# A hybrid decoder step on one core: the prompt's compressed rows computed ahead of the fourth gate chunk

## The chip, the cores and the metric

One core of one Trainium2 chip runs the whole kernel. The metric is the device time of one execution in microseconds; the kernel before takes 467.59 us (median of 3 runs, 466.97 to 469.56).

## The reference

One layer of a hybrid decoder, for a prompt of 512 tokens and for 8 sequences that decode one token each. Every token's row is normalised and multiplied by one matrix `w_in`; the columns feed a state-space head group (32 groups with a scan over time) and an attention head group (8 query heads, 2 key/value heads). The attention has three branches: over compressed rows, over selected blocks and over a sliding window. Both groups are gated, joined, and multiplied by an output matrix. The compressed rows are made thus:

```python
def compress(rows, pe, w1, b1, w2):
    B, L, G, HD = rows.shape
    ch = rows.reshape(B, L // CMP_STRIDE, CMP_STRIDE, G, HD)
    pe = pe.reshape(2, CMP_STRIDE, 1, HD)
    w1 = w1.reshape(2, CMP_STRIDE, HD, CMP_HID)
    pa = jnp.einsum('bnjgd,jdh->bngh', ch + pe[0], w1[0])
    pb = jnp.einsum('bnjgd,jdh->bngh', ch + pe[1], w1[1])
    hid = jax.nn.gelu(pa[:, :-1] + pb[:, 1:] + b1)
    return jnp.einsum('bngh,hd->bngd', hid, w2)
```

It is done once for the prompt's own keys and values, and once, with the same weights, for the 1024 past tokens of each of the 8 decode sequences, which lie in a paged cache and are fetched through a page table.

## The kernel before

**Stages.** The first phase (`dense` and `ssm_all`, merged) normalises the input and multiplies it by `w_in` in chunks: u, five chunks of queries, keys and values, and last four gate chunks (`gate_mm`, each of some 190 matmuls of 128x256 or 128x264, three matmuls to a product since both operands are split in a high and a low part). The state-space runs of four sequences' worth of groups (`ssm_run`, sq 0 to 3) lie among them; their last matmuls are L782 and L787, their transposes at the end L810 and L811. The second phase merges `prompt` (four query/key tiles, attention, the GLU of the state-space output) and `sample` (compression and attention for the decode sequences, in four pairs). The third is the output projection.

**What sets the order.** A tile scheduler places every engine's instructions from the program's order, which it takes as the priority, and from its own estimate of when operands and buffers come free. Each engine then runs its list strictly in order, and waits at the head of the list until the operands are there.

**The compression of the prompt** (`compress_prompt`) is the first thing that `sample` does. It loads the weights `W1r` (four tiles of 512 KB), splits them in `W1h` (a cast on ScalarE) and `W1l` (a subtraction on VectorE, 1024 columns each), reads the prompt's key and value rows back from the output in DRAM as `ch` (four loads, L1108), transposes them on TensorE (L1113, eight 128x128), copies them to `XP`, multiplies by `W1r` (L1123, 128 matmuls; `kd` 0 for keys, then `kd` 1 for values), adds a bias `hb`, takes a GELU (`gx`, with results in `hidp`) and multiplies by `w2` (L1133, L1141). `pen` (L1101 transposes it) is the position embedding, laid out behind the rows in `XP`.

**Shared buffers.** The raw weights `W1r` lie in the pool `ld` of four buffers. The cache gathers of the decode sequences (tile `kvg`, L1329, one indirect DMA each on GpSimd) take their buffers from the same pool, so that the first four gathers need the four `W1r` tiles read for the last time. Of a gathered page VectorE makes `xr`, GpSimd copies `Vs`, TensorE transposes the keys (L1338) and `xr` (L1348), which becomes `XT`; L1372 multiplies it by `W1h` and `W1l`. `gx` and the tile `qsv` share a pool of two buffers.

**The query/key tiles** (`qk_tile`): `qs` and `ks` are split (ScalarE and VectorE), transposed on TensorE (L995, L1002), and ScalarE writes them to `QT` and `KT`. `QB` and `KN` are the decode sequences' queries and keys (L967, L969; scores L1286), L1291 spreads the gates.

Of the kernel before, what the change touches and what calls it, by code (L numbers as in the profile page):

```python
# [8 lines left out]
F32 = mybir.dt.float32  # L9
F32R = mybir.dt.float32r  # L10
# [26 lines left out]
def hymba_step_kernel(  # L37
# [87 lines left out]
    def run(*gens):  # L125
        for g in gens:
            for _ in g:
                pass
# [768 lines left out]

    def ssm_all():
        tab = ssm_tables(0)
        yield 1  # L900
        for sq in range(4):
            nxt = ssm_tables(sq + 1) if sq < 3 else None
            yield 1
            ssm_run(sq, tab)
            tab = nxt
            yield 1
        ssm_states()

    def dense():
# [40 lines left out]
        yield 1  # L950
        run(gate_mm(2, Wg[2]))
        yield 1
        run(gate_mm(3, Wg[3]))

# [99 lines left out]


    cw = cache_win[0]

    def load_w1(tile_):

        r = [[tile_("W1r") for _ in range(2)] for _ in range(2)]  # L1060
        for kd in range(2):
            for a in range(2):
                nc.sync.dma_start(r[kd][a].rearrange("p (j h) -> p j h", h=128),
                                  cmp_w1[0, kd, 1024 * a:1024 * a + 1024].rearrange("(j r) h -> r j h", r=128))
        return r

    w2 = st([128, 2, 64], "w2", tag="pni")
    nc.sync.dma_start(w2, cmp_w2[0].rearrange("k h d -> h k d"))
    pen = k1("pen", 128, 32)
    nc.sync.dma_start(pen, cmp_pe[0].rearrange("k (a j) d -> (k a) (j d)", j=2))  # L1070
    hb = st([128, 2], "hb")
    GC = math.sqrt(2.0 / math.pi)

    def gelu2(out, pin, n, bias):

        xb, x2 = k3("gx"), k3("gx2")
        for kd in range(2):
            S.activation(xb[:, n * kd:n * kd + n], pin(kd), AF.Identity, bias=bias[:, kd:kd + 1])
        xx, yy = xb[:, :2 * n], x2[:, :2 * n]
        S.activation(yy, xx, AF.Square)  # L1080
        V.tensor_scalar(yy, yy, 0.044715, 1.0, op0=ALU.mult, op1=ALU.add)
        V.tensor_tensor(yy, yy, xx, op=ALU.mult)
        S.activation(yy, yy, AF.Tanh, scale=GC)
        V.scalar_tensor_tensor(out, yy, 1.0, xx, op0=ALU.add, op1=ALU.mult)


    kcT = st([128, 2, 2, 32], "kcT", F32R)
    vbd = st([128, 2, 4, 64], "vbd", tag="Dm")

    W1h = [[None] * 2 for _ in range(2)]  # L1090
    W1l = [[None] * 2 for _ in range(2)]

    def compress_prompt():
        W1r = load_w1(ld)
        for kd in range(2):
            for a in range(2):
                W1h[kd][a], W1l[kd][a] = wh("W1h"), wh("W1l")
                split(W1h[kd][a], W1l[kd][a], W1r[kd][a])
        peT = k1("peT", 32)
        p = pb("cmp")  # L1100
        T.transpose(p[:, :32], pen, ident[:32, :32])  # L1101
        V.tensor_copy(peT, p[:, :32])
        XPv = [k2("XP", 528).rearrange("p (j n) -> p j n", n=66) for _ in range(2)]
        for kd in range(2):
            V.tensor_copy(XPv[kd][:, :, 64:66], peT[:, 16 * kd:16 * kd + 16].rearrange("p (a j) -> p j a", j=8))
        ch = pt_("ch")
        for kg in range(4):
            nc.sync.dma_start(ch[32 * kg:32 * kg + 32].rearrange("p (j d) -> p j d", d=64),  # L1108
                              kvp_rows[:, 64 * kg:64 * kg + 64].rearrange("(c j) d -> c j d", j=16))
        for hf in range(2):  # L1110
            p = pb("cmp")
            for j in range(4):
                T.transpose(p[:, 128 * j:128 * j + 128], ch[:, 512 * hf + 128 * j:512 * hf + 128 * j + 128], ident)  # L1113
            for kd in range(2):
                V.tensor_copy(XPv[kd][:, 4 * hf:4 * hf + 4, 0:64],
                              p.rearrange("p (j k n) -> p j k n", k=2, n=64)[:, :, kd, :])
        ph = pb("cmp")
        for kd in range(2):
            for jp in range(8):
                for a in range(2):  # L1120
                    for c in range(2):
                        o = 128 * jp + 64 * c
                        T.matmul(ph[64 * c:64 * c + 64, 65 * kd:65 * kd + 65], W1r[kd][a][:, o:o + 64], XPv[kd][:, jp, a:a + 65],  # L1123
                                 start=(kd == 0 and jp == 0 and a == 0), stop=(jp == 7 and a == 1), skip_group_check=True,
                                 tile_position=(0, 64 * c))
            yield 1
        V.tensor_tensor(hb, ph[:, 64:130:65], b1T, op=ALU.add)
        hidp = k1("hidp")
        gelu2(hidp, lambda kd: ph[:, 65 * kd:65 * kd + 64], 64, hb)
        V.memset(vbd, 0.0)  # L1130
        pk = pb("cmp")
        for e in range(2):
            T.matmul(pk[64 * e:64 * e + 64, 0:64], w2[:, 0, :], hidp[:, 0:64], start=True, stop=True, tile_position=(0, 64 * e))  # L1133
# [624 lines left out]
```

## Time and profile before

| what | value |
|---|---|
| median of 3 runs | 467.59 us (466.97 to 469.56) |
| profiled execution | 468.64 us, span 466.9 us |
| mean granted TensorE clock | 0.985 |
| TensorE busy | 452.1 us (97%) |
| VectorE, ScalarE, GpSimd busy | 348.8, 241.3, 95.4 us |
| chain that ended last, by engine | PE 73%, DVE 13%, DMA 7%, POOL 3% |

Times are microseconds from the span's start. PE is TensorE's matmul stream, DVE VectorE, ACT ScalarE, POOL GpSimd, SP the engine that issues most DMAs. A row of a timeline gives the start, the time from there to the last end, engine, line, operation, tiles, the number of instructions, and in brackets the idle time of that engine just before it and what ended it. Matmuls overlap, so the times of rows next to each other do not add up to the stretch that they cover. The chain of waits is followed back from the last instruction; its pieces do add up.

### The profile page before, as it was taken

The page shows a single profiled execution, that of the slowest core. Times are in us where ns is not written, and L with a number is a line of the kernel's source. Part 1 is how long each engine was busy: PE and PEld are TensorE (multiplying, and loading weights), DVE is VectorE, ACT ScalarE, POOL GpSimd, SP SyncE. Part 2 cuts the span into 40 slices and gives each one's busy share as a digit, 9 for nine tenths or more (in the row PEclk, how much of TensorE's full clock was granted, in tenths as well). Part 3 has the DMA queues.
Part 4 walks back from the last instruction along what each step waited for, and adds up shares of the span by engine and source line. Part 5 has one row for each costly group of instructions (what it writes and reads, how often), then busy time and mean ns, then how long its engine had stood idle before and what let it go on. Part 6 is the DMA issues. An engine that isn't in the chain of part 4 may idle for free.

```text
span 466.9 us, 10954 instructions
## 1 busy us (share of the span) xinstructions
PE 452.1 (97%) x4258; PEld 385.9 (83%) x4258; DVE 348.8 (75%) x942; ACT 241.3 (52%) x587; POOL 95.4 (20%) x104
## 2 busy tenths in 40 slices
PE   8999999999999998799999999999899999999996
PEld 4989999899999998698686776867568799799885
DVE  6978999998998998385676858687756687683332
ACT  5913764756324328475676668566856555342100
POOL 3100000056442000462342214321433010000000
PEclk9999999999999997789999999999999999999999
DMA  8776533614627433466143362429343784311211
GB/s 290 247 225 167 84 73 108 187 40 82 143 57 214 129 82 73 148 209 187 46 140 114 121 215 79 148 90 350 104 141 130 220 209 152 101 58 58 69 46 48
DMA packets 75635, 62.84 MB, mean 135 GB/s; under 512 B 29262, under 2 KB 69056, under 8 KB 75456
## 3 DMA queue, kind: packets, MB, share of 16 engines
q1 hardware_dynamic: 66208, 36.74, 28.2%
q0 software_dynamic: 4816, 17.03, 11.5%
q10 hardware_dynamic: 4560, 8.39, 5.7%
q8 instruction: 33, 0.54, 0.5%
q14 instruction: 18, 0.15, 0.1%
HBM read 55.63 MB, written 10.70 MB: 142 GB/s over the span
## 4 chain that ended last, share of the span: by engine, by line
PE 73%; DVE 13%; DMA 7%; POOL 3%; issue 2%; ACT 1%; SPq 0%; DVEq 0%; POOLq 0%; ACTq 0%
PE a L121 11%; PE a L122 11%; PE a L123 10%; PE ph L1372 8%; DMA kvg<-in_cache_kv_dram,idx 4%; PE a L1262 4%; PE t L1253 4%; PE a L1220 3%; PE t L1348 3%; PE c L1545 3%; POOL rsq L168 2%; DVE ga L62 2%; PE t L1338 2%; PE ph L473 1%; DMA x<-in_x_prompt_dram 1%
## 5 line engine op out<-in xcount | busy, mean ns | idle before, releaser
L121 PE MATMUL a<-hTh,whi 128*128 128x256 f32 (+1 forms) x192 | 54.8, 287 | 0.6 <-DVE sg L61 0.6
L122 PE MATMUL a<-hTh,wlo 128*128 128x256 f32 (+1 forms) x192 | 54.8, 287 | 0.0
L123 PE MATMUL a<-hTl,whi 128*128 128x256 f32 (+1 forms) x192 | 53.4, 284 | 0.0
L1329 POOL DMA_INDIRECT kvg<-in_cache_kv_dram,idx x32 | 32.8, 1026 | 82.2 <-PE c L1123 40.1
L168 POOL TENSOR_TENSOR rsq<-rsq,mhalf 128x6 f32<-128x6 f32 (+3 forms) x10 | 28.7, 2872 | 101.8 <-DVE rsq L62 101.8
L122 PE MATMUL a<-whi,hTl 128*128 128x256 f32 (+1 forms) x160 | 45.8, 287 | 0.0
L123 PE MATMUL a<-wlo,hTh 128*128 128x256 f32 (+1 forms) x160 | 45.3, 284 | 0.0
L121 PE MATMUL a<-whi,hTh 128*128 128x256 f32 (+1 forms) x160 | 45.2, 287 | 0.0
L1372 PE MATMUL ph<-XT,W1h 128*128 128x256 f32 x256 | 44.5, 298 | 0.0
L61 ACT ACTIVATE P<-a,mx 128x128 f32<-128x128 f32 (+3 forms) x64 | 33.6, 533 | 13.3 <-DVE mx L61 11.5
L61 DVE TENSOR_REDUCE mx<-a 128x1 f32<-128x384 f32 (+3 forms) x48 | 27.9, 596 | 13.8 <-PE a L1221 13.6
L121 PEld LDWEIGHTS a<-hTh,whi 128*128 128x128 f32 x192 | 36.2, 188 | 1.1 <-DVE sg L61 0.8
L122 PEld LDWEIGHTS a<-hTh,wlo 128*128 128x128 f32 x192 | 36.2, 188 | 0.9 <-issue 0.4
L122 PE MATMUL a<-woh,mixl 128*128 128x256 f32 x128 | 36.1, 283 | 0.0
L121 PE MATMUL a<-woh,mixh 128*128 128x256 f32 x128 | 36.1, 284 | 0.0
L123 PE MATMUL a<-wol,mixh 128*128 128x256 f32 x128 | 36.0, 283 | 0.0
L123 PEld LDWEIGHTS a<-hTl,whi 128*128 128x128 f32 x192 | 35.7, 189 | 0.1
L1372 PEld LDWEIGHTS ph<-XT,W1h 128*128 128x128 f32 x256 | 34.9, 192 | 0.3 <-ACT XT L61 0.2
L62 ACT CAST whi<-w 128x1024 fp32r<-128x1024 f32 (+4 forms) x26 | 23.9, 927 | 15.8 <-PE a L122 10.5
L61 ACT COPY pT<-t 128x512 f32<-128x512 f32 x40 | 23.1, 588 | 15.8 <-PE t L1253 12.6
L122 PEld LDWEIGHTS a<-whi,hTl 128*128 128x128 f32 x160 | 30.1, 188 | 1.2 <-issue 0.9
L121 PEld LDWEIGHTS a<-whi,hTh 128*128 128x128 f32 x160 | 29.9, 189 | 0.9 <-PE ph L473 0.4
(410 smaller groups left out, 1235.5 us busy)
## 6 DMA issues: line engine op xcount, KB each, us to landing
w<-in_w_in_dram SPq DMA_DIRECT2D x16, 512.0 KB
out_dram<-in_cache_win_dram ACTq DMA_DIRECT2D x8, 511.0 KB
x<-in_x_prompt_dram SPq DMA_DIRECT2D x4, 512.0 KB
TT<-scr_k SPq DMA_DIRECT2D x4, 512.0 KB
w<-in_w_in_dram SPq DMA_DIRECT2D x16, 128.0 KB
W1r<-in_cmp_w_dram SPq DMA_DIRECT2D x4, 512.0 KB
wk<-in_cache_win_dram SPq DMA_DIRECT2D x8, 256.0 KB
wv<-in_cache_win_dram SPq DMA_DIRECT2D x8, 256.0 KB
```

The lines of the kernel that those rows point to most:

```text
L61: return f(*args, **kw)
L62: return f(*args, **kw)
L121: T.matmul(out, ah, bh, start=start, stop=False, skip_group_check=True)
L122: T.matmul(out, al, bh, start=False, stop=False, skip_group_check=True)
L123: T.matmul(out, ah, bl, start=False, stop=stop, skip_group_check=True)
L168: return G.tensor_tensor(out, out, mhalf[:parts, :cols], op=ALU.pow)
L1220: T.matmul(bank, QTv(g, r)[:, qsl], KTv(g, a)[:, brs, :n], start=(a == 0), stop=False, skip_group_check=True)
L1253: T.transpose(p[:, 128 * r:128 * r + 128], P[r][:, br, 128 * kt:128 * kt + 128], ident)
L1262: mm = T.matmul(po[64 * br:64 * br + 64, :], kvt[kt - 1][:, c0:c0 + 64], behind[kt - 1][br][0], start=(kt == 1), stop=(kt == i + 1), tile_ ...
L1329: G.indirect_dma_start(out=gt_, out_offset=None, in_=ckv, in_offset=bass.IndirectOffsetOnAxis(ap=idx[:, 2 * pr_ + b2, jq:jq + 1], axis=0))
L1348: T.transpose(p[:, 256 * g + 128 * b2:256 * g + 128 * b2 + 128], gts[jq][b2][:, o:o + 128], ident)
L1372: T.matmul(ph3[:, kd], (W1l if part == 1 else W1h)[kd][a][:, wsl], (xl if part == 2 else xh)[:, e, a:a + 256], start=(jq == 0 and kd == 0 ...
```

## The change

`load_w1`, `gelu2`, `compress_prompt`, the loads of `w2` and `pen` and their tiles stand ahead of `ssm_all` and `dense`. The splits are a function of their own, `w1_split`. `dense` loads `W1r` ahead of gate chunk 2, runs the compression to its end after that chunk, and splits the weights of `kd` 1 after gate chunk 3; those of `kd` 0 are split inside the compression, after its first 64 matmuls. `sample` takes three empty turns in its place. Nothing is computed that was not computed before. Lines of the changed kernel: L1093, L1100 were L995, L1002; L955 was L1113; L965 was L1123; L977, L985 were L1133, L1141; L1065, L1067 were L967, L969; L1291, L1296 were L1286, L1291; L1343, L1353, L1377 were L1338, L1348, L1372.

```diff
+    def w1_split(W1r, kd):
+        for a in range(2):
+            W1h[kd][a], W1l[kd][a] = wh("W1h"), wh("W1l")
+            split(W1h[kd][a], W1l[kd][a], W1r[kd][a])
+
+    def compress_prompt(W1r):
...
+        ph = pb("cmp")
+        for kd in range(2):
+            for jp in range(8):
+                for a in range(2):
+                    for c in range(2):
...
+            if kd == 0:
+                w1_split(W1r, 0)
+            yield 1
...
+        W1r = load_w1(ld)
         run(gate_mm(2, Wg[2]))
+        run(compress_prompt(W1r))
         yield 1
         run(gate_mm(3, Wg[3]))
+        w1_split(W1r, 1)
...
-    def compress_prompt():
-        W1r = load_w1(ld)
-        for kd in range(2):
-            for a in range(2):
-                W1h[kd][a], W1l[kd][a] = wh("W1h"), wh("W1l")
-                split(W1h[kd][a], W1l[kd][a], W1r[kd][a])
...
     def sample():
-        yield from compress_prompt()
+        yield 1
+        yield 1
+        yield 1
         for i in range(4):
             yield from sample_pair(i)
```

The diff does not tell where the scheduler puts the moved instructions. On TensorE around the transposes of `ch`, the list before (a row is line, operation, output and inputs with buffer numbers, size, and how many alike):

```order
L1002 MATMUL a_3000<-identr_303,ks_2988 128x128 x4
L1101 MATMUL c_2826<-cst_70,pen_2753 128x32
L995 MATMUL a_3037<-identr_303,qs_2985 128x128 x4
L1113 MATMUL c_2838<-cst_70,ch_2833 128x128 x4
L1113 MATMUL c_2845<-cst_70,ch_2833 128x128 x4
L1002 MATMUL a_3044<-identr_303,ks_2988 128x128 x4
L995 MATMUL a_3074<-identr_303,qs_3066 128x128 x4
L1123 MATMUL c_2852<-XP_2829,W1r_2801 64x65 x2
L1123 MATMUL c_2852<-XP_2829,W1r_2802 64x65 x2
```

And the list of the changed kernel, from the last matmul of gate chunk 3 (L123) on:

```order
L123 MATMUL a_2820<-hTl_115,whi_2469 128x264
L1093 MATMUL a_2957<-identr_303,qs_2949 128x128 x4
L1100 MATMUL a_2964<-identr_303,ks_2952 128x128 x4
L955 MATMUL c_2649<-cst_70,ch_2644 128x128 x3
L810 MATMUL t_2511<-cst_70,hfin_486 16x128
L811 MATMUL t_2511<-cst_70,hs_485 128x128
L810 MATMUL t_2511<-cst_70,hfin_486 16x128
L811 MATMUL t_2511<-cst_70,hs_485 128x128
L955 MATMUL c_2649<-cst_70,ch_2644 128x128
L955 MATMUL c_2656<-cst_70,ch_2644 128x128 x4
L1093 MATMUL a_2971<-identr_303,qs_2949 128x128 x4
L1100 MATMUL a_2978<-identr_303,ks_2952 128x128 x4
```

The first transposes of `ch` stand behind two groups of four transposes of the query/key tiles, in place of seven. Behind these rows come five more transposes of `qs` and `ks`, and then the 128 matmuls L965 in one piece. All of it still follows gate chunk 3; the state-space matmuls L782 and L787 of sq 3 now stand 33 matmuls ahead of that chunk's end.

On TensorE around the first gathered pages, the list before:

```order
L1002 MATMUL a_3081<-identr_303,ks_3069 128x128 x3
L995 MATMUL a_3092<-identr_303,qs_3066 128x128 x4
L1002 MATMUL a_3099<-identr_303,ks_3069 128x128 x4
L1338 MATMUL t_3013<-cst_70,kvg_3014 128x128 x2
L995 MATMUL a_3144<-identr_303,qs_3136 128x128 x4
L1348 MATMUL t_3030<-cst_70,xr_3017 128x128
L1002 MATMUL a_3151<-identr_303,ks_3139 128x128 x4
L1338 MATMUL t_3013<-cst_70,kvg_3021 128x128 x2
L995 MATMUL a_3166<-identr_303,qs_3136 128x128 x4
L1348 MATMUL t_3030<-cst_70,xr_3024 128x128
L1348 MATMUL t_3030<-cst_70,xr_3017 128x128
```

And that of the changed kernel:

```order
L1100 MATMUL a_3099<-identr_303,ks_3069 128x128 x4
L1093 MATMUL a_3144<-identr_303,qs_3136 128x128 x4
L1100 MATMUL a_3151<-identr_303,ks_3139 128x128 x4
L977 MATMUL c_2748<-hidp_2737,w_496 64x64 x2
L985 MATMUL c_2755<-w_496,hidp_2737 32x64 x8
L1093 MATMUL a_3166<-identr_303,qs_3136 128x128 x4
L1065 MATMUL t_2883<-cst_70,qsv_2884 128x8 x4
L1067 MATMUL t_2883<-cst_70,kvs 128x8 x2
L1343 MATMUL t_3013<-cst_70,kvg_3014 128x128 x2
L1343 MATMUL t_3013<-cst_70,kvg_3021 128x128 x2
L1100 MATMUL a_3173<-identr_303,ks_3139 128x128 x4
L1353 MATMUL t_3030<-cst_70,xr_3017 128x128
```

The query/key tiles that stood between and behind the `L1123` rows now follow `L965`, and the matmuls of `hidp` (L977, L985), which stood well behind the first L1372, stand ahead of the transposes of the gathered pages `kvg_3014` and `kvg_3021`.

On VectorE from the bias `hb` on, before:

```order
L61 TENSOR_TENSOR hb_2755<-c_2852,spT_320 128x2
L62 COPY xr_3017<-kvg_3014 128x2x4x64
L62 COPY xr_3024<-kvg_3021 128x2x4x64
L61 COPY kT_3028<-t_3013 128x512
L62 TENSOR_SCALAR gx_2956<-gx_2956 128x128
L62 TENSOR_TENSOR gx_2956<-gx_2956,gx_2955 128x128
L62 COPY xr_3110<-kvg_3107 128x2x4x64
L61 TENSOR_TENSOR XT_2789<-t_3030,XT_2787 128x2x256
L62 COPY xr_3117<-kvg_3114 128x2x4x64
L62 SCALAR_TENSOR_TENSOR hidp_2954<-gx_2956,gx_2955 128x128
```

And of the changed kernel:

```order
L61 TENSOR_TENSOR hb_500<-c_2663,spT_320 128x2
L62 COPY xr_3017<-kvg_3014 128x2x4x64
L62 COPY xr_3024<-kvg_3021 128x2x4x64
L62 TENSOR_TENSOR ks_3139<-kvt_312,ks_3139 128x2x128 x2
L62 TENSOR_SCALAR gx_2739<-gx_2739 128x128
L62 TENSOR_TENSOR gx_2739<-gx_2739,gx_2738 128x128
L62 SCALAR_TENSOR_TENSOR hidp_2737<-gx_2739,gx_2738 128x128
L62 COPY qsv_2884<-qsr_316 8x512
L62 MEMSET vbd_502 128x512
L61 COPY QB_2880<-t_2883 64x4x4 x4
L61 COPY KN_2882<-t_2883 128x16
```

The GELU's two steps and `hidp` still stand behind the copies `xr` of the first two gathered pages, but `qsv`, `vbd`, `QB`, `KN` and the key copy `kT` now stand behind `hidp`. On GpSimd the first four gathers come ahead of the copies `Vs`, and the fifth and sixth behind all four; on SP the four loads of `ch` keep their place among the stores `scr_y`. From the first L1372 of `jq` 2 on (at 213.36 us in the trace before) TensorE's list is the same in both kernels, and so it is on the other engines from about there.

## Rows read from the trace of the kernel before

**Rows 1.** The chain of waits around the phases' boundary: start, us on the chain, what.

```profile
177.92 0.61 DVE qs L62
...
187.59 1.14 PE c L1123 x32
...
188.94 2.97 PE c L1123 x96
...
192.17 5.88 DMA kvg<-in_cache_kv_dram,idx
...
204.16 0.27 PE c L1133 x4
204.42 0.38 PE c L1141 x16
```

**Rows 2.** Timeline of PE, 173 to 215 us.

```profile
175.20 2.16 PE L787 MATMUL t<-U,TT 128*64 128x72 f32 x32
178.58 0.54 PE L995 MATMUL a<-identr,qs 128*128 128x128 f32 x4 [1.22 <-DVE qs L62]
...
179.38 0.42 PE L1002 MATMUL a<-identr,ks 128*128 128x128 f32 x3
...
184.69 1.93 PE L1113 MATMUL c<-cst,ch 128*128 128x128 f32 x8
...
195.73 0.69 PE L1338 MATMUL t<-cst,kvg 128*128 128x128 f32 x2 [2.77 <-DMA kvg<-in_cache_kv_dram,idx]
...
200.90 0.91 PE L1372 MATMUL ph<-XT,W1h 128*128 128x256 f32 x4
...
213.36 0.72 PE L1372 MATMUL ph<-XT,W1h 128*128 128x256 f32 x4
```

**Rows 3.** Stretches: length, busy us of each engine, then PEclk (granted clock), DMA share.

```profile
181.00:187.30 6.30, 6.30 (x56) 5.93 (x54) 4.56 (x24) 5.38 (x19) 0.00 (x0) 0.50 0.23 49
187.30:195.00 7.70, 5.66 (x143) 5.19 (x141) 2.22 (x7) 3.51 (x14) 3.30 (x4) 0.94 0.29 82
195.00:201.20 6.20, 4.96 (x29) 4.78 (x30) 3.20 (x7) 3.20 (x10) 4.04 (x6) 0.50 0.75 251
201.20:213.40 12.20, 12.20 (x123) 11.14 (x121) 10.60 (x23) 7.69 (x23) 5.32 (x8) 0.99 0.66 198
```

**Rows 4.** Timelines of DVE, ACT and POOL, the same stretch.

```profile
176.71 1.22 DVE L62 TENSOR_TENSOR W1l<-W1r,W1h 128x1024 fp32r<-128x1024 f32 x1
...
188.61 0.75 DVE L62 TENSOR_TENSOR ks<-kvt,ks 128x256 fp32r<-128x256 f32 x2
...
198.07 0.43 DVE L62 COPY xr<-kvg 128x512 f32<-128x512 f32 x1 [1.94 <-DMA kvg<-in_cache_kv_dram,idx]
...
199.43 0.48 DVE L62 TENSOR_SCALAR gx<-gx 128x128 f32<-128x128 f32 x1
199.94 0.50 DVE L62 TENSOR_TENSOR gx<-gx,gx 128x128 f32<-128x128 f32 x1
...
201.78 0.48 DVE L62 SCALAR_TENSOR_TENSOR hidp<-gx,gx 128x128 f32<-128x128 f32 x1
```

```profile
193.25 0.66 ACT L61 CAST QT<-a 128x256 fp32r<-128x256 f32 x2
193.76 0.70 ACT L61 CAST KT<-a 128x256 fp32r<-128x256 f32 x2
...
200.95 0.33 ACT L62 ACTIVATE gx<-gx 128x128 f32<-128x128 f32 x1
```

```profile
190.78 1.09 POOL L1329 DMA_INDIRECT kvg<-in_cache_kv_dram,idx  x1 [40.12 <-PE c L1123]
192.17 0.96 POOL L1329 DMA_INDIRECT kvg<-in_cache_kv_dram,idx  x1 [0.30 <-DVE hb L61]
```

**Rows 5.** SP's queue at the boundary, and two direct loads on the chain.

```profile
174.67 2.70 SPq L1108 DMA_DIRECT2D ch<-out_dram  x3
```

```profile
147.03 4.14 DMA W1r<-in_cmp_w_dram
...
151.59 1.95 DMA out_dram<-kvt
```

More of the change, by code (lines that the diff above doesn't have):

```diff
@@ L895, in silu_gates, with load_w1 @@
             yield 1
+    cw = cache_win[0]
+    def load_w1(tile_):
+        r = [[tile_("W1r") for _ in range(2)] for _ in range(2)]
+        for kd in range(2):
+            for a in range(2):
+                nc.sync.dma_start(r[kd][a].rearrange("p (j h) -> p j h", h=128),
+                                  cmp_w1[0, kd, 1024 * a:1024 * a + 1024].rearrange("(j r) h -> r j h", r=128))
+        return r
+    w2 = st([128, 2, 64], "w2", tag="pni")
+    nc.sync.dma_start(w2, cmp_w2[0].rearrange("k h d -> h k d"))
@@ new lines, in hymba_step_kernel, with gelu2 @@
+    pen = k1("pen", 128, 32)
+    nc.sync.dma_start(pen, cmp_pe[0].rearrange("k (a j) d -> (k a) (j d)", j=2))
+    hb = st([128, 2], "hb")
+    GC = math.sqrt(2.0 / math.pi)
+    def gelu2(out, pin, n, bias):
+        xb, x2 = k3("gx"), k3("gx2")
+        for kd in range(2):
+            S.activation(xb[:, n * kd:n * kd + n], pin(kd), AF.Identity, bias=bias[:, kd:kd + 1])
+        xx, yy = xb[:, :2 * n], x2[:, :2 * n]
+        S.activation(yy, xx, AF.Square)
+        V.tensor_scalar(yy, yy, 0.044715, 1.0, op0=ALU.mult, op1=ALU.add)
+        V.tensor_tensor(yy, yy, xx, op=ALU.mult)
+        S.activation(yy, yy, AF.Tanh, scale=GC)
+        V.scalar_tensor_tensor(out, yy, 1.0, xx, op0=ALU.add, op1=ALU.mult)
@@ L1053, in glu @@
                 V.scalar_tensor_tensor(mixS[:, ct], th[:, 0:8], 0.25, sgS[0][:, ct], op0=ALU.mult, op1=ALU.mult)
-    cw = cache_win[0]
-    def load_w1(tile_):
-        r = [[tile_("W1r") for _ in range(2)] for _ in range(2)]
-        for kd in range(2):
-            for a in range(2):
-                nc.sync.dma_start(r[kd][a].rearrange("p (j h) -> p j h", h=128),
-                                  cmp_w1[0, kd, 1024 * a:1024 * a + 1024].rearrange("(j r) h -> r j h", r=128))
-        return r
@@ L1067, in hymba_step_kernel @@
[L1067 to L1084, printed above, removed]
@@ L1087, in hymba_step_kernel @@
[L1087 to L1091, printed above, removed]
-    def compress_prompt():
-        W1r = load_w1(ld)
-        for kd in range(2):
-            for a in range(2):
-                W1h[kd][a], W1l[kd][a] = wh("W1h"), wh("W1l")
-                split(W1h[kd][a], W1l[kd][a], W1r[kd][a])
[L1099 to L1133, printed above, removed]
-        kcs = k1("kcs", 64)
-        S.mul(kcs, pk[:, 0:64], 0.5)
-        V.tensor_copy(kcT[:, :, 0, :], kcs.rearrange("p (g c) -> p g c", g=2))
-        V.tensor_tensor(kcT[:, :, 1, :], kcs.rearrange("p (g c) -> p g c", g=2), kcT[:, :, 0, :].bitcast(F32), op=ALU.subtract)
-        pk = pb("cmp")
-        for r in range(4):
-            for g in range(2):
-                T.matmul(pk[32 * r:32 * r + 32, 64 * g:64 * g + 64], hidp[:, 64 + 32 * g:64 + 32 * g + 32], w2[:, 1, :],
-                         start=(g == 0), stop=(g == 1), skip_group_check=True, tile_position=(0, 32 * r))
-        for r in range(4):
-            sl = slice(32 * r, 32 * r + 32)
-            S.mul(vbd[sl, :, r, :], pk[sl, 0:128].rearrange("p (g d) -> p g d", g=2), 0.5)
-        yield 1
@@ L1671, in sample @@
     def sample():
-        yield from compress_prompt()
+        yield 1
+        yield 1
+        yield 1
         for i in range(4):
```

47 lines of the change are left out of this document (added).

## The prediction

> **What bounds the kernel now.** I read the chain of waits first. The change moves work at the boundary of the first two phases, and there the chain changes hands: VectorE's split `qs` [rows 1], then TensorE through L1123, then one gather of 5.88 us, then TensorE again to the end. The second view is TensorE's timeline: L787 ends the first phase at 175.20 + 2.16 = 177.36, the engine is idle for 1.22 us for `qs`, does transposes and L1123, is idle for 2.77 us for the second gathered page, and starts the first L1372 at 200.90 [rows 2]. The third is the table of stretches, for the clock: after each of these two idles the granted clock stood at 0.50, the lower level, first for 181.0 to 187.3, then for 195.0 to 201.2, and TensorE was busy in all or most of both [rows 3]. From 201.2 to 213.4 it is busy without a gap (12.20 of 12.20 us) at 0.99. The fourth is GpSimd's timeline: the first gather is issued at 190.78 after 40.12 us of idleness that L1123 ends, and the second at 192.17 [rows 4]. They wait for the weights' raw buffers.
>
> From the L1372 at 213.36 [rows 2] on the lists of both kernels agree and TensorE is full, so whatever is won or lost by then is carried to the end at about its size. The sum is therefore a question of one number: when the first L1372 (call it T0, 200.90 before) starts, and what work has by then been done in advance.
>
> **The change, step by step.**
>
> *The boundary.* One of the four splits `W1l` (1.22 us [rows 4]) no longer stands ahead of the first `qs` on VectorE. `qs` can be ready at about 177.3, when L787 and the gate matmuls end, and the 1.22 us of idleness shrink to 0 to 0.5. TensorE begins the query/key tile at 177.4 to 177.9 in place of 178.58. The split comes later, beside transposes; it gates only the later gathers.
>
> *The transposes of `ch`.* They now stand behind two groups of transposes. Twelve transposes took from 178.58 to 179.80 [rows 2], 0.1 each, so they are at the head of the queue at 178.2 to 178.7. The loads of `ch` keep their place: the three last are issued from 174.67 to 177.37 [rows 5], the last of them from about 176.5. The trace does not show when it lands. The nearest direct loads on the chain took 1.95 us (another small transfer) and 4.14 us (512 KB) [rows 5]; `ch` has a quarter of the bytes, so I take it near the lower, at 178.9, and keep 178.4 to 180.6. In the kernel before this landing was covered by seven us of other work (177.4 to 184.69 [rows 2]); that cover is gone. The wait at the head of the queue is then 0 to 2.4 us, and I take about 0.5.
>
> *L965.* From the first L1113 to the first L1123 the kernel before took 2.9 us, at the low clock [rows 1, 2]. After, 25 transposes at 0.1 lie there, and the copies to `XP`; I keep the 2.9. L965 starts at 181.8. The 32 matmuls took 1.14 us [rows 1], so the 64 of `kd` 0 end at 184.1 and all 128 near 186.
>
> *The gathers.* Before, the 64th matmul ended at 188.94 + 32 x 0.031 = 189.9, and the first gather followed at 190.78, 0.85 later, the second 1.39 after that [rows 1, 4]. After: 185.0 and 186.4. The second lands 5.88 later, at 192.2, against 198.05: the transfer that the kernel waits for is nearly 6 us earlier.
>
> *What is late next.* This gain doesn't reach T0. The matmuls of `hidp` (L977, L985) now stand ahead of the first page's transposes on TensorE, and `hidp` is made on VectorE behind the copies `xr` of the first two pages. After the landing at 192.2 follow xr 0.43, `ks` 0.75, gx 0.48 and 0.50, tanh 0.33 on ScalarE, hidp 0.48 [rows 4], 2.97 in all. L977 starts at 195.2, with both pages' transposes queued behind it, though the pages have long been there. TensorE has less than that to do: nine groups of transposes follow L965, which ScalarE empties at 0.51 a pair of copies [rows 4], so they end by about 190.8. Some four us of idleness remain until 195.2.
>
> *From L977 to T0.* 20 transposes at 0.1, 0.65 for L977 and L985 [rows 1], some 0.75 for the small matmuls of the decode queries and gates (an estimate: they are few, each below a transpose), 0.5 for the last copy to `XT`: 3.9 us at full clock, 199.1, and 3.4 more at half, 202.5. The rows say low: both idles above a microsecond were followed by a low stretch, which began 2.0 us (192.96 to 195.0) or 3.6 us (177.36 to 181.0) after the idle's start and lasted 6.2 or 6.3 us [rows 2, 3]. From an idle near 191 that is low from 193 to 194.6, until 199.2 to 200.9. L977 and what follows run at half until then. I take T0 = 201.0, with 199.9 to 202 as bounds.
>
> *The sum.* T0 moves by +0.1, and 0.65 for the `hidp` matmuls, which before came behind T0, is already done: -0.55. The sum stands against the profiled execution, 468.64 (span 466.9 and 1.74 around it): 468.1. That execution lies 1.05 above the median of the runs, so the forecast is 467.0; the bounds of T0 give 465.9 to 468.0. The moved small loads, the empty turns and the earlier `hfo`, `hso` copies cost nothing as long as TensorE's list covers them; if that cover goes, they are below half a microsecond each. A difference under 0.5% (2.34 us) is about what a measurement here can't tell from no change.
>
> **The rivals.**
>
> *A, faster: the clock is high when L977 comes.* The idle may be split up by the late `qs` and `ks` tiles, or the low stretch may end early. For it: 1.22 us of idleness at the boundary is gone, and with it, it may be, the first low stretch. Against it: both long idles of this trace cost a low stretch. Then T0 = 199.1, -1.8 - 0.65 = -2.45: 465.1, and down to 464 if gathers land faster than 5.88.
>
> *B, slower: `ch` lands late.* Place: the first L955, at the head of TensorE's list. If `ch` lands after about 179.9, TensorE idles for over 1.2 us, the idle that before was followed by 6.3 us at half [rows 2, 3]. Then L965's `kd` 0 takes 4.6 in place of 2.3, and with the wait the second gather lands 3.5 to 4.7 later, at 195.7 or after; L977 starts at 198.7, still behind `hidp`, and a second low stretch follows. T0 near 204.6: +3.7 - 0.65 = +3.0, 470.6. For it: a third of the landing's bounds lies beyond that point. Against it: the transfer is small.
>
> *C, slower: transposes do not hold the clock.* TensorE does 33 transposes between the gate chunk and L965 and some 35 after it. If they did not count as work, the clock would fall in the first of these stretches whatever `ch` does, and the time would be that of B, 470.6. The rows speak against it: the clock rose at 187.3 after 6.3 us of 56 matmuls that are nearly all transposes [rows 3]. The Trainium skill, TensorE: Matmul & The Clock Gate, Part 4 (PE-mode transpose), states that the full clock does not engage for transposes, since they are not counted as busy. By that rule the change would be slower; by the row, it is not decided by transposes, and this trace disagrees with the page.
>
> *D, nothing:* the scheduler keeps the compression behind gate chunk 3, so its words promise more than its list holds; if the gathers gain nothing either, 467.6.
>
> **How the numbers follow.** The forecast, -0.55, gets 0.45: every step rests on a row but the landing of `ch`. A gets 0.28, B 0.16, C 0.06, D 0.05. Faster by over 0.5% is A, 0.28; within is the forecast and D, 0.50; slower is B and C, 0.22. The range goes from within A (464.6) to B's time (470.6); left out are the far half of B and C and a tail of A. The likeliest case alone holds 465.9 to 468.0.
>
> **What would show it.** Right: the second gather issued near 186.4 and landing near 192; TensorE idle for some four us ahead of L977, released by `hidp`; a clock of 0.50 behind that; the first L1377 near 201. An idle ahead of L955 over 1.2 us and 0.50 during L965 would show B; the same without the idle, C. No idle ahead of L977 would make the whole sum wrong, and so would a stretch behind T0 where TensorE has gaps.

## The result, and the profile after

The changed kernel takes 470.87 us (median of 12 executions, 470.18 to 473.1), the kernel before 467.8 (12 executions, 465.68 to 469.56). The ratio is 1.0066, with a 95% interval of 1.0045 to 1.0087: slower by 3.1 us, where 0.55 faster was forecast, and outside the range. The time lies at that of the rivals B and C (470.6), but it will turn out that neither mechanism is what happened. Ratios, and the rows for the kernel before in the table below, leave out the few executions that took over 1.5% longer than the fastest of their kernel.

The chain of waits of the changed kernel around the boundary, the pieces that the prediction had priced:

```profile
172.99 3.25 DMA ch<-out_dram
...
185.60 6.06 DMA kvg<-in_cache_kv_dram,idx
...
192.98 0.15 DVE gx L62
193.15 0.38 DVE gx L62
193.55 0.32 ACT gx L62
193.89 0.30 DVE hidp L62
194.24 0.48 PE c L977 x4
```

By the chain one of the three late loads of `ch` landed at 172.99 + 3.25 = 176.24, and L955, which reads all four loads, did not wait at 177.85. The second gather was issued at 185.60 (forecast 186.4, before 192.17 [rows 4]) and took 6.06 us. From its landing the chain goes where the prediction put it: VectorE's steps to `hidp`, and L977 at 194.24 (forecast 195.2).

The timeline of TensorE:

```profile
176.62 0.28 PE L123 MATMUL a<-hTl,whi 128*128 128x264 f32 x1
176.97 0.54 PE L1093 MATMUL a<-identr,qs 128*128 128x128 f32 x4
...
177.85 0.52 PE L955 MATMUL c<-cst,ch 128*128 128x128 f32 x3
...
181.11 3.95 PE L965 MATMUL c<-XP,W1r 128*64 128x65 f32 x128
...
186.94 0.53 PE L1093 MATMUL a<-identr,qs 128*128 128x128 f32 x4 [0.79 <-ACT KT L61]
...
192.70 0.70 PE L1100 MATMUL a<-identr,ks 128*128 128x128 f32 x3 [1.25 <-DVE ks L62]
194.24 0.48 PE L977 MATMUL c<-hidp,w 128*64 128x64 f32 x4 [0.84 <-DVE hidp L62]
...
201.61 1.22 PE L1377 MATMUL ph<-XT,W1h 128*128 128x256 f32 x4
...
215.97 0.74 PE L1377 MATMUL ph<-XT,W1h 128*128 128x256 f32 x4
```

The 1.22 us of idleness at the boundary [rows 2] are gone, and L965 runs at full clock. The idleness ahead of L977 is 2.1 us, where some four were forecast, and in two pieces: 1.25 for the split `ks`, which stands behind the copies `xr` on VectorE as `hidp` does, and 0.84 for `hidp`. T0, the first L1377, is at 201.61 (forecast 201.0, before 200.90). Up to here the sum holds to 0.6 us. Then comes what it did not hold: the L1372 that stood at 213.36 [rows 2] now starts at 215.97, 2.6 us later, though the 0.65 us of `hidp` matmuls were done in advance. The table of stretches says why (length, busy us of each engine, clock, DMA share; the last two rows are the single microseconds in which the clock fell and rose):

```profile
177.00:185.00 8.00, 7.50 (x162) 7.05 (x162) 7.33 (x20) 6.38 (x19) 1.05 (x1) 1.00 0.27 55
185.00:190.90 5.90, 3.65 (x34) 2.95 (x31) 0.59 (x2) 4.58 (x17) 3.77 (x5) 0.99 0.73 238
190.90:194.20 3.30, 1.25 (x6) 0.74 (x5) 2.09 (x6) 0.77 (x4) 1.09 (x2) 0.50 0.57 215
194.20:207.60 13.40, 13.36 (x98) 12.02 (x99) 8.99 (x30) 7.07 (x22) 3.80 (x5) 0.50 0.26 81
207.60:213.40 5.80, 5.80 (x53) 5.17 (x52) 2.71 (x6) 3.96 (x16) 1.90 (x2) 0.98 0.41 142
...
190.00:191.00 1.00, 0.80 (x8) 0.62 (x7) 0.00 (x0) 1.00 (x4) 0.00 (x0) 0.89 0.93 266
207.00:208.00 1.00, 1.00 (x8) 1.00 (x7) 0.93 (x3) 0.00 (x0) 0.00 (x0) 0.58 0.00 0
```

The first low stretch of the kernel before is gone: the clock is 1.00 from 177 to 190.8. But the second one starts there and lasts until 207.8, 17.1 us; those of before, read in steps of a microsecond, lasted 6.8 each. For 13.4 us of it TensorE is fully busy at half rate. The clock fell ahead of the waits for `ks` and `hidp`, behind five idles of 0.2 to 0.8 us between the groups of transposes; the waits lie inside the low stretch.

Of the 2.6 us at 215.97 the profiled executions keep 1.5 to the end (spans of 468.4 and 466.9): behind that row TensorE idles 1.2 us less than before. The medians are 3.1 apart because the profiled execution of the kernel before lies above its median and that of the changed kernel below its own.

One profile could be an accident, so the mean granted clock of the single executions is set beside it. Time x (1 - clock) estimates what the low clock took, as if TensorE were busy throughout, and the rest is what the kernel would take at full clock. The clock, what it took and the rest are means over the executions; those of the kernel before come from the five sets of the experiments.

| kernel (executions) | median us | mean clock | low clock took | rest |
|---|---|---|---|---|
| before (17 to 30 in each of five sets) | 467.5 to 468.9 | 0.986 to 0.987 | 6.0 to 6.8 | 461.6 to 462.2 |
| changed (12) | 470.87 | 0.978 | 10.4 | 460.8 |

The clock takes some 4 us more in the changed kernel, and the rest is about 1 us lower; the two make the 3.1 by construction. The estimate books half of any idle time at the low clock under the clock; TensorE idled for 2.1 us of the low stretch of the changed kernel and for 1.7 us of those of before, which nearly cancels between these two, but not everywhere.

### The profile page after: what moved, and what is told of

The parts are those of the page before. It is cut to its first block, busy times and chain, and to the rows that moved or that the text cites. A ratio compares the mean times of both kernels' runs of the same rounds, so it can differ in the third digit from the quotient of the medians.

```text
span 468.4 us, 10955 instructions
## 1 busy us (share of the span) xinstructions
PE 454.9 (97%) x4258; PEld 387.5 (83%) x4258; DVE 348.0 (74%) x942; ACT 240.9 (51%) x587; POOL 93.8 (20%) x104
## 4 chain that ended last, share of the span: by engine, by line
PE 77%; DVE 9%; DMA 8%; issue 2%; ACT 1%; SPq 1%; POOL 1%; POOLq 0%; DVEq 0%; ACTq 0%
PE a L122 13%; PE a L121 13%; PE a L123 12%; PE ph L1377 8%; PE a L1267 4%; PE t L1258 3%; DMA kvg<-in_cache_kv_dram,idx 3%; PE a L1225 3%; PE t L1353 3%; DMA yT<-scr_y 2%; PE c L1550 2%; PE t L1343 2%; PE ph L473 1%; DVE ga L62 1%; DMA x<-in_x_prompt_dram 1%
## 5 line engine op out<-in xcount | busy, mean ns | idle before, releaser
L123 PE MATMUL a<-hTl,whi 128*128 128x256 f32 (+1 forms) x192 | 53.5, 284 | 0.0
L168 POOL TENSOR_TENSOR rsq<-rsq,mhalf 128x6 f32<-128x6 f32 (+3 forms) x10 | 27.1, 2715 | 101.6 <-DVE rsq L62 101.6
L1377 PE MATMUL ph<-XT,W1h 128*128 128x256 f32 x256 | 45.7, 303 | 0.0
L123 PE MATMUL a<-wlo,hTh 128*128 128x256 f32 (+1 forms) x160 | 45.3, 284 | 0.0
L123 PE MATMUL a<-wol,mixh 128*128 128x256 f32 x128 | 36.0, 283 | 0.0
L1377 PEld LDWEIGHTS ph<-XT,W1h 128*128 128x128 f32 x256 | 35.5, 194 | 0.5 <-ACT XT L61 0.2
L123 PEld LDWEIGHTS a<-hTl,whi 128*128 128x128 f32 x192 | 35.8, 188 | 0.0
L123 PEld LDWEIGHTS a<-wlo,hTh 128*128 128x128 f32 x160 | 30.1, 188 | 0.2 <-issue 0.2
```

The costliest lines, as they stand in the source:

```text
L123: T.matmul(out, ah, bl, start=False, stop=stop, skip_group_check=True)
L168: return G.tensor_tensor(out, out, mhalf[:parts, :cols], op=ALU.pow)
L1377: T.matmul(ph3[:, kd], (W1l if part == 1 else W1h)[kd][a][:, wsl], (xl if part == 2 else xh)[:, e, a:a + 256], start=(jq == 0 and kd == 0 ...
```

## The experiments

The first theory: the gain of the earlier gathers is lost in the wait for `hidp`, and in the low clock around it. The following kernels tested it.

**qsv in another pool.** In the changed kernel `gx` holds both buffers of the pool k3 until `hidp` is made, so `qsv`, and with it `QB` and `KN`, come behind `hidp`. One word moves it:

```diff
-    qsv = k3("qsv", 512, 8).rearrange("p (r g d) -> p r g d", r=4, g=2)
+    qsv = k2("qsv", 512, 8).rearrange("p (r g d) -> p r g d", r=4, g=2)
```

> The changed kernel with one word different: qsv takes a buffer of the pool k2 in place of k3, where gx holds both buffers until hidp is made. The list of TensorE then has the first pages' transposes (L1343) ahead of the matmuls of hidp (L977, L985), which fall behind the first L1377. Theory 1 (the gain of the earlier gathers is lost in the wait of TensorE's list for hidp, 192.70 to 194.24 in the changed kernel, and in the long low stretch of the clock behind it, 190.9 to 207.6): the first L1377 starts at 194 to 197 in place of 201.61, the low stretch is shorter than 12 us, and the time is 465 to 468. Rival (the loss comes from the gathers that collide or from the later ones, or from the divided splits): the time stays at 470 to 471.5, whatever the order of L977 and L1343.

Measured: 465.06 us (8 executions), ratio to the kernel before 0.9928 (0.9903 to 0.9953); mean clock 0.994, so that the low clock took 2.9 us and the rest is 462.4. Its timeline of TensorE and its stretches:

```profile
190.53 0.44 PE L1343 MATMUL t<-cst,kvg 128*128 128x128 f32 x2 [2.75 <-DMA kvg<-in_cache_kv_dram,idx]
...
192.53 0.55 PE L1343 MATMUL t<-cst,kvg 128*128 128x128 f32 x2 [0.83 <-DMA kvg<-in_cache_kv_dram,idx]
...
196.01 0.77 PE L1377 MATMUL ph<-XT,W1h 128*128 128x256 f32 x4
...
200.43 0.34 PE L977 MATMUL c<-hidp,w 128*64 128x64 f32 x4
```

```profile
185.00:191.00 6.00, 3.25 (x77) 3.04 (x74) 2.24 (x10) 2.96 (x11) 4.38 (x5) 1.00 0.49 161
191.00:196.60 5.60, 4.77 (x34) 4.37 (x33) 4.10 (x10) 3.66 (x12) 3.74 (x6) 0.70 0.79 277
196.60:206.60 10.00, 10.00 (x121) 8.95 (x119) 7.44 (x21) 7.44 (x23) 4.40 (x6) 1.00 0.59 188
```

T0 is 196.01, 5.6 us earlier than in the changed kernel, with the gathers no earlier (the second at 187.07); L977 stands behind it. The low stretch is 3.4 us. The rival falls: the first gathers still come together and early, the splits stay divided, and the loss is gone. By the estimate of the table the gain over the kernel before lies in the clock (2.9 us for 6.0 to 6.8), and the rest is no lower than before; what the early gathers brought by themselves is not shown.

The same kernel on another chip:

> The changed kernel with qsv in the pool k2 once more, on the chip of this set, since its time is the lowest of the study and rests on 8 executions: 464.5 to 466.5, ratio to the kernel before 0.990 to 0.996. If it had been that chip's doing: 467 to 469.

465.11 us (12 executions), ratio 0.9957 (0.993 to 0.9984). Its two medians are the lowest of all versions here; by its ratio this second one is not apart from the 0.9955 of a version further down.

**The same pool change in the kernel before.**

> The kernel before, with qsv in the pool k2 as in the run that gave 465.06. It tells whether that gain belongs to qsv's pool alone. Theory 1 (the pool matters only where gx holds both buffers of k3 before qsv is made, which is so in the changed kernel alone): 467 to 469, as before. Rival (qsv alone is the gain): 464.5 to 466.

471.45 us (6 executions), ratio 1.0078 (1.0047 to 1.0109): slower, which neither theory had. The order shifts here too: TensorE waits 1.11 us for ScalarE's `QT` at the boundary, the gathers are issued later (the first at 193.61 against 190.78 [rows 4]), and the first L1372 starts at 203.09 in place of 200.90. So 465.06 is not `qsv`'s gain alone; it needs the moved compression.

**The second half of the compression put back.** The bias, the GELU and the `hidp` matmuls become the first step of `sample` again; loads and L965 stay early.

```diff
+    def compress_tail():
+        ph = phc[0]
         V.tensor_tensor(hb, ph[:, 64:130:65], b1T, op=ALU.add)
...
     def sample():
-        yield 1
         yield 1
         yield 1
+        yield from compress_tail()
```

> The changed kernel with the second half of the compression (hb, the GELU, the matmuls of hidp, kcT, vbd) put back as the first step of sample; loads, L965 and the divided splits stay early. The matmuls of hidp (L983, L991) then stand behind the first L1383, but five groups of query/key transposes ahead of L965. Theory 1: no wait for hidp ahead of the first pages; gathers about 1 to 2 us later than in the changed kernel; the first L1383 at 195 to 198; time 465 to 468.5. Rival (early gathers, divided splits or later gathers cost): 470 to 471.5.

468.22 us (12), ratio 0.9989 (0.9968 to 1.001), mean clock 0.987; the second gather at 186.96, the first L1383 at 197.10. All within what theory 1 said. It undoes the loss, and no more; its low stretch in the profile is 10.2 us.

**The divided splits alone.** The weights loaded and split as in the change, the compression computed in `sample` (the splits of `kd` 0, which lie inside it, go with it).

> The divided splits alone: weights loaded and split as in the changed kernel (those of kd 1 behind gate chunk 3), the compression computed in sample as before. Theory 1: as the kernel before, or better by the 1.22 us idle for qs at the boundary: 465.5 to 468. If the divided splits are what costs: 469.5 to 471.5.

467.81 us (12), ratio 0.998 (0.9952 to 1.0007). **All splits ahead of the compression**, the other way about:

> The changed kernel with all four splits ahead of the compression, as before the change; the list of TensorE is the same from gate chunk 3 on. Theory 1 (the divided splits cost and bring nothing by themselves): 470 to 471.5. If dividing the splits brings what the change has of gain, it is slower by the 1.22 us of the split ahead of qs: 471.5 to 472.5; if dividing them costs, 468 to 469.5.

471.13 us (12), ratio 1.0059 (1.003 to 1.0089); its first `qs` waits for the split again (W1l at 175.95, qs at 177.09) and its first L1376 starts at 201.63, as in the changed kernel. The division of the splits neither costs nor brings anything that can be measured.

**hidp ahead of the pages.** The wait is taken away, on VectorE:

```diff
+                if pr_ == 0 and jq == 0:
+                    with tc.issue_after(hid0[0].ins):
+                        xc()
```

Here `xc` is the copy `xr` of a page and `hid0[0]` the instruction that makes `hidp`.

> The changed kernel with one order added on VectorE: the copies xr of the first two pages come behind hidp. hidp then doesn't wait for the pages. Theory 1, its part on the wait: hidp is ready at 190 to 192 in place of 194.18, the idle ahead of L977 is gone or below 0.5, the first pages' transposes start at 193 to 195 and the time is 466 to 469.5. If the clock falls all the same (idles between the query/key groups remain, some 3 us from 186 to 192) and small matmuls follow, the low stretch may still be 8 us or more and the time stays near 469.5. Rival (not the wait): 470 to 471.5.

467.57 us (12), ratio 0.9998 (0.9977 to 1.0018): 3.3 us below the changed kernel, about what the change had cost. L977 starts without a wait:

```profile
191.09 0.48 PE L977 MATMUL c<-hidp,w 128*64 128x64 f32 x4
```

The edit takes away both pieces of the wait, that for `ks` too. The clock falls at 190.7 all the same, so the wait did not set the fall off, but it is back after 6.8 us in place of 17.1. (This profiled execution, 465.22 us at a mean clock of 0.993, is the fastest of the twelve; the others have 0.982 to 0.985, and so more low clock.) Over the executions the mean clock is 0.985 in place of 0.978, the low clock took 6.9 us in place of 10.4, and the rest is 460.9, the same as in the changed kernel. So most of what the wait cost, it cost by what the clock did; the estimate books about a microsecond of the idleness itself under the clock. TensorE's list is the same up to L985. Behind that it differs: ahead of the clock's return two groups stand earlier, and behind it the scores L1169 and L1226 come ahead of the first L1383. So the run takes away the wait and changes that order together.

**Keeping TensorE busy ahead of L977.** In the changed kernel, 34 matmuls of no use are added after the query/key groups (by the table of stretches TensorE is idle for 4.3 us there, not for the 4.9 of the expectation):

```diff
+            for _ in range((0, 0, 0, 6, 8, 16, 4, 0)[2 * i + g]):
+                T.matmul(pwd[:, 0:256], identr, QTv(g, 0)[:, 0:256], start=True, stop=True)
```

> The changed kernel with 34 additional matmuls of 128x256 (identr by QT, into an unused bank, about 0.11 us each at full clock, 3.9 us in all) in TensorE's list between L965 and L977, where TensorE was idle for 4.9 us. They add work and compute nothing that is used. Theory 1, its part on the clock: with TensorE kept busy until L977 the clock stays at 1.00 past 191, the matmuls from L977 to row 207 run at full, and the first L1377 of jq 2 comes 3 to 6 us earlier than 215.97; time 465 to 468. Rival (the wait alone costs, or the low clock comes from transposes and small matmuls whatever the idle): the clock falls all the same, and the time is 470 to 473.

470.65 us (12). The clock did change: the mean is 0.988, the low clock took 5.6 us in place of 10.4, and its fall comes at 196.5 in place of 190.8. The time lies in the rival's range all the same. `hidp` was still late (L977 at 194.87 behind 1.99 us of idleness), the clock fell behind that, and a last query/key tile and the scores L1172 to L1230 moved ahead, so that the first L1381 starts at 204.97. The gain on the clock was given back, 3.9 us of it to the added matmuls (the estimate of the expectation); on the time the run decides nothing.

The same without the wait: 16 such matmuls in the kernel that has `hidp` first, whose order is otherwise nearly the same.

> The run with hidp ahead of the copies xr, plus 16 matmuls of 128x256 (some 0.11 us each) in one place of TensorE's list, where idles of 0.2 to 0.6 us lay between the groups of transposes (187 to 190); TensorE's order is the same but for a swap of two groups. Without them that run's clock fell at 190.8, had a mean of 0.985 over its executions, and took 467.57. Theory 3 (the idles ahead of the fall set it off: transposes that ScalarE empties too slowly at full clock): the clock falls later or not at all, mean clock 0.990 or above, time 464.5 to 466.5 though 1.8 us of work are added. Rival (the small matmuls from L977 on pull the clock down whatever lies ahead): mean clock 0.983 to 0.987, time 467.5 to 469.

466.85 us (12), just above the range expected, ratio 0.9955 (0.9931 to 0.9979), mean clock 0.992: the low clock took 3.7 us in place of 6.9, with 1.8 us of work added. In time the two versions lie 0.7 us apart and were measured in different sets; the intervals of their ratios overlap. The stretches without and with the 16 matmuls, first the kernel without them:

```profile
185.00:191.00 6.00, 4.67 (x51) 3.74 (x45) 1.76 (x7) 5.17 (x21) 3.88 (x5) 0.97 0.70 219
191.00:196.60 5.60, 5.60 (x61) 4.73 (x60) 4.19 (x13) 5.18 (x17) 2.43 (x4) 0.50 0.38 146
196.60:206.60 10.00, 10.00 (x88) 8.93 (x87) 8.06 (x25) 6.46 (x23) 4.06 (x5) 0.95 0.48 149
```

and with them:

```profile
185.00:191.00 6.00, 5.81 (x83) 5.42 (x79) 1.86 (x6) 4.06 (x16) 4.54 (x5) 1.00 0.63 188
191.00:196.60 5.60, 4.41 (x67) 3.72 (x66) 3.71 (x13) 5.43 (x20) 1.78 (x4) 0.97 0.50 189
196.60:206.60 10.00, 9.99 (x50) 9.03 (x49) 6.86 (x21) 4.92 (x17) 3.70 (x5) 0.51 0.35 107
```

TensorE is busy 5.81 of 6 us from 185 to 191 in place of 4.67, and the clock stays up there; in this execution, the slowest of its twelve, it fell later, behind an idle of 1.13 us for `qsv`. So the fall at 190.8 goes with the idles ahead of it, in which TensorE waits for ScalarE to empty the transposes: with that place filled, the mean clock of twelve executions is higher. That filling them shortens the kernel is not shown beyond the 0.7 us.

**Transposes as the filling.** The added matmuls were plain ones, so that the run above can't tell idles from transposes that do not hold the clock, the prediction's rival C. Here 20 transposes stand in the same place:

```diff
-                T.matmul(pwd[:, 0:256], identr, QTv(g, 0)[:, 0:256], start=True, stop=True)
+                T.transpose(pwd[:, 0:128].bitcast(F32R), QTv(g, 0)[:, 128:256], identr)
```

> As the run with hidp ahead of the copies xr and 16 added matmuls of 128x256 (466.85, mean clock 0.992), but what is added at that place is 20 transposes of 128x128, which lie among transposes. It tells idles from transposes. Theory 3 (the idles ahead of the fall set it off): the fall is put off as with the matmuls, mean clock 0.989 or above, time 465.5 to 467.5. Rival C of the prediction (transposes do not hold the clock, so that nine groups of them and 20 more let it fall whatever the idles are): mean clock 0.983 to 0.986 as without any filling, time 468 to 469.5.

Mean clock 0.993 (12 executions): the low clock took 3.4 us. Transposes held it as well as matmuls. The time is 468.13, ratio 1.0015 (0.9986 to 1.0044), above what theory 3 expected and in the range of its rival: what the clock gave was lost elsewhere, since the rest is 464.8 in place of 460.9 (1.9 us of it are the added transposes). Nor do idles alone decide: in the profiled execution TensorE was busy for less of the stretch ahead of L977 than where the clock fell (4.32 of 6 us against 4.67), 1.53 us of the idleness in one piece, and the clock stayed at 1.00:

```profile
185.00:191.00 6.00, 4.32 (x55) 3.97 (x51) 1.65 (x5) 3.71 (x14) 3.83 (x5) 1.00 0.70 243
```

In this execution the clock is 0.999 on the mean, and a later wait comes instead: TensorE idles for `XT`, and VectorE's `xr` copies, from which it is made, wait 2.4 us for gathered pages in that stretch:

```profile
213.10 0.74 PE L1387 MATMUL ph<-XT,W1h 128*128 128x256 f32 x4 [2.25 <-DVE XT L61]
```

**Small matmuls in the low stretch.** A second theory was that L985, L1291 and L1296, small matmuls behind L977, keep the clock from returning. Eight transposes of 8x8, or four of 128x128, were added ahead of each of the first two groups of L1353 in the version with qsv in k2:

```diff
+            if pr_ == 0 and jq == 0:
+                for _ in range(8):
+                    T.transpose(p[0:8, 0:8], gts[0][1][0:8, 0:8], ident[0:8, 0:8])
```

> The kernel with qsv in k2 and the change, with 16 additional transposes of 8x8 (some 0.05 us each, 8 ahead of each of the first two groups of L1353), in the low stretch of 192.9 to 196.1. They compute nothing that is used. Theory 2 (small matmuls in a low stretch put off the return of the clock): the low stretch lasts 6 us or more in place of 3.2, and the time is 467 to 469. Rival (the return comes whatever the matmuls are): 3 to 4 us low, and the time 465 to 466.5.

> The control of the run with 16 small transposes: at the same two places 4 transposes of 128x128 each, about as much time (8 at 0.1 to 0.2 us). Theory 2: the low stretch stays at 3 to 4 us, and the time is 465 to 466.5. If additional work of any kind puts off the return of the clock: 6 us or more low, 467 to 469.

466.52 us (10) with the small ones and 467.04 (10) with the wide ones; the low clock took 4.5 and 4.0 us, against 2.9 without either, and the stretches in the profiles are 10.2 and 6.8 us. The two differ by less than their executions scatter (465.53 to 469.55 and 465.55 to 469.81), so that nothing shows the small ones to be worse than the wide ones. The wide ones' time lies in the range set for additional work of any kind. In the changed kernel three sets of small matmuls were cut, L985 as shown here and L1291 and L1296 likewise:

```diff
-        for r in range(4):
-            for g in range(2):
-                T.matmul(pk[32 * r:32 * r + 32, 64 * g:64 * g + 64], hidp[:, 64 + 32 * g:64 + 32 * g + 32], w2[:, 1, :],
...
+        T.matmul(pk[:, 0:128], hidp, w2.rearrange("p k d -> p (k d)"), start=True, stop=True)
```

> The changed kernel, its order unchanged, with three sets of small matmuls in the low stretch cut to one matmul each: L985 (8 to 1), the decode queries' scores L1291 (8 to 1) and the gates' spreading L1296 (4 to 1). What is left out is most of these products, so the compressed values, those scores and those gates are not computed. In the changed kernel they took 0.61, 0.52 and 0.97 us on the chain; some 1.8 us of that goes at the low clock. Theory 2 (the small matmuls in the low stretch put off the return of the clock): the mean clock goes from 0.978 to 0.984 or above, and the time to 465.5 to 468. Rival (the wait for hidp and the idles ahead of it set the length): the mean clock stays at 0.977 to 0.982, and the time is 468.5 to 470, lower by the work left out alone.

470.0 us (12), ratio 1.0025 (0.9993 to 1.0058), median clock 0.978 as before the cut (mean 0.981; the low clock took 8.9 us for 10.4), the low stretch in the profile 20.5 us, with 0.50 in all of this:

```profile
191.00:196.60 5.60, 4.71 (x31) 4.11 (x32) 2.94 (x8) 4.74 (x19) 1.46 (x3) 0.50 0.46 184
196.60:206.60 10.00, 10.00 (x49) 8.88 (x49) 7.60 (x26) 5.32 (x18) 3.65 (x4) 0.50 0.33 107
```

The time is 0.9 us below the changed kernel by the medians, which are of different sets, and 1.9 by the ratios to the kernel before (1.0025 and 1.0066), about the 1.8 us of work left out. Clock and time lie in the rival's ranges. The small matmuls are not the main cause; the second theory falls. In this profile TensorE waits only 0.77 us ahead of L977, and not for `ks`, and yet the stretch is the longest of all, so that the length of the wait does not set the length of the stretch.

**Both mends.** qsv in k2 and hidp ahead of the pages:

> Both mends in one: qsv in k2, and hidp ahead of the copies xr of the first pages. If the two costs are separate, it is below the 465.06 of qsv in k2 alone: 463.5 to 465. But the list of TensorE has L977 again ahead of the first L1383, and behind it the small matmuls L1292, L1297 and L1169: if the wait for hidp is gone by either mend, the second adds nothing, and 465 to 467.5 is expected.

466.6 us (12), ratio 0.9966 (0.9941 to 0.999), mean clock 0.992. The second mend adds nothing to the first, and the first L1383 is back at 200.62: with `hidp` early, L977, the compressed scores L1169 and the first L1226 stand ahead of it again.

## Why the prediction was wrong

Step by step, as it put them:

- *The boundary*: right. The idle for `qs` went from 1.22 us to nothing, L1093 starts at 176.97.
- *The transposes of `ch`*: right in the outcome. I feared a landing between 178.4 and 180.6; a load issued at 172.99 landed at 176.24, since the three loads were issued some 2.3 us earlier (from 172.33), and L955 ran at 177.85 without a wait. Rival B's condition never came up: TensorE was not idle there, and L965 ran at 1.00.
- *L965 and the gathers*: right, 0.7 and 0.8 us early (181.11 for 181.8, 185.60 for 186.4).
- *What is late next*: right in its order. `hidp` behind the copies of both pages, L977 ahead of the pages' transposes, L977 at 194.24, a microsecond early. The idleness was 2.1 us for the four forecast, and more of it was for `ks` (1.25) than for `hidp` (0.84). Taking `hidp` and `ks` out of that place gave back 3.3 us.
- ***From L977 to T0* is the step that failed.** It took the length of the low stretch, 6.2 to 6.3 us (6.8 by finer steps), from the two of the kernel before, "until 199.2 to 200.9". The length was 17.1 us. The start was 2 to 4 us early, at 190.8 for 193 to 194.6, and not behind the idle that was to set it off but ahead of it. T0 itself hardly shows this (201.61 for 201.0), by luck: L977 came a microsecond early, and the way from it to T0 took 7.4 us, all at half rate, for the 5.8 charged. But the 6.2 us behind T0, up to 207.8, were to run at full rate, and ran at half. For the L1372 of 213.36 the sum amounts to 212.8; it came at 215.97, and of these 3.2 us 0.6 stand ahead of T0 and 2.6 behind it. The sentence "whatever is won or lost by then is carried to the end at about its size" holds from 213.36 on but roughly (1.5 of 2.6 us in the profiles), and the sum that stopped at T0 stopped too early: a stretch that begins ahead of T0 need not end with it.

Over the executions the low clock takes 10.4 us where the kernel before has 6.0 to 6.8, so that the low stretch was mis-sized by enough to make it some 4 us more. The rest of the sum (-0.55) stands beside a measured rest of about -1, which is no finer than the estimate behind it.

Two smaller readings were off and changed nothing of this. Of the 56 matmuls between 181.0 and 187.3, 24 are L1286 and L1291 and not transposes; transposes alone are what ran from 183.22 to L1123 at 187.52, just ahead of the clock's rise. And the small matmuls of the decode queries and gates, put at 0.75 us at full clock, took 2.2 at half rate on the chain.

- *Rival A* (faster, clock high when L977 comes) did not come up: the late `ks` did split the idle, but the clock was at 0.50 from 190.8 on. Where L977 did run at the high clock, with 16 matmuls or 20 transposes added, the time was 466.85 and 468.13. A time of 465.1 came with another order (qsv in k2, T0 at 196.01, L977 behind it), which is not this rival.
- *Rival B* had the time, 470.6, by luck: its mechanism, the late `ch`, did not occur.
- *Rival C*, transposes do not hold the clock, falls. In the version with qsv in k2 TensorE ran transposes alone from 192.53 to 196.01, and the clock rose from 0.50 to 1.00 at 196.1; and 20 added transposes raised the mean clock from 0.985 to 0.993. The Trainium skill, TensorE: Matmul & The Clock Gate, Part 4 (PE-mode transpose), has it that the full clock does not engage for transposes. For their f32 transposes of 128x128 the runs of this case disagree with the page.
- *Rival D*, nothing gained by the gathers, did not come up: the first two were issued 6.8 and 6.6 us earlier (183.95 and 185.60).

What is shown: the loss goes when `hidp` no longer waits behind the pages' copies ahead of L977, or when L977 no longer stands ahead of the pages' transposes (four versions, 465.1 to 468.2 us), and what goes with it is low clock. Filling the idles between the groups of transposes raised the mean clock too, but hardly moved the time. What stays open: why the clock stayed at 0.50 for 13.4 us in which TensorE was busy 13.36. Small matmuls, transposes and the divided splits are ruled out as the main cause; the wait and the order behind L985 changed together and were not told apart.

## What to carry to other kernels

Bringing a wait's end forward by 6 us is worth only what stands next in the waiting engine's list: look there for an instruction whose inputs come by another road, here a matmul of a GELU whose steps queue behind the very data that came early. A gap of a microsecond or two on TensorE is to be priced with the low clock that may follow, and the length of such a stretch seen once is not a price: 3.4 to 20.5 us were seen here, and in one execution idles of 1.53 and 2.25 us were followed by none. An estimate needs both ends of the stretch. Where pools order a program, a buffer shared with an unrelated tile can hold a whole branch; one word, another pool, turned 3.1 us more into 2 to 3.4 us less than the kernel before (ratios 0.9957 and 0.9928), and the same word alone made the kernel before slower (1.0078).

## What the runs showed of the hardware that I had not expected

- The low clock can last long under full load: 0.50 for 13.4 us at 13.36 us busy. The whole stretch was 17.1 us there, and 17.1 and 20.5 in the two versions with the same order (all splits ahead, small matmuls cut); in the profiles of the other versions the low stretches of this part were 3.4 to 10.2 us, and one had none.
- The mean clock differs between executions of one kernel, from 0.976 to 0.996 in the kernel before, and the time from 464.5 to 471.6. A single profile of the clock decides little: the profiled execution of the small transposes was the slowest of its ten.
- The clock came back to 1.00 behind 3.5 us of transposes alone (192.53 to 196.01), and with 20 transposes added among others it stayed there.
